# The order of the split buffers in the last column of a down stage

## The chip, the cores and the metric

The kernel runs on one core of a Trainium2 chip. The metric is the device time of one execution in microseconds; before the change it is 1727.62 us, the median of 3 runs (1727.11 to 1728.93). Times below are microseconds from the start of the profiled span unless marked otherwise.

## What is computed

One decoder layer on x of 256 rows (tokens) and 2048 columns, all float32: a feed-forward block (FFN 1), a mixer, a second feed-forward block (FFN 2), and a final norm. The two FFNs are alike, and they are what the change touches:

```python
def swiglu_ffn(x, w_gate, w_up, w_down):
    return (jax.nn.silu(x @ w_gate) * (x @ w_up)) @ w_down

x = x + 0.5 * swiglu_ffn(rms_norm(x, ffn1_norm[l]), ffn1_w_gate[l], ffn1_w_up[l], ffn1_w_down[l])
...
x = x + y @ w_out[l]
x = x + 0.5 * swiglu_ffn(rms_norm(x, ffn2_norm[l]), ffn2_w_gate[l], ffn2_w_up[l], ffn2_w_down[l])
return rms_norm(x, final_norm)
```

w_gate and w_up are 2048 x 5632, w_down is 5632 x 2048. Between the FFNs stands the mixer: one input projection (2048 x 5120), a gated recurrence in one half of the columns, a gated short convolution in the other, and an output projection.

## The kernel before

**Splitting.** Each weight tile is loaded as float32 (a raw tile), then split into a high part, rounded by ACT (`act.copy`, seen as CAST hi), and a low part, raw minus high, by VectorE (TENSOR_TENSOR lo). TensorE multiplies with both: of a unit of four blocks of 128 rows by 512 columns, each of the two row tiles t takes 8 matmuls with the high part and 4 with the low part, 24 in all. `parts_of` (line 259) does a split in one piece, `low_part` (252) the low part alone.

**Pairs.** The high and low tile of one split are a pair. There are three pairs while the layout is "three", two in the layouts "two" and "fine" (line 187 on). Each pair is a pool of its own, allocated one after the other on the left side of SBUF: in "three" a pair has four blocks (8 KB high and 8 KB low per partition), in "fine" five blocks (10 KB and 10 KB). A stage opens its pools when the one before has closed its own, at the same base address, so the fine stage's pair0 lies over all of the pair0 of "three" and over the first 4 KB of its pair1's high tile; the fine pair1 lies over the rest of pair1 and over the high tile of pair2. A new tile waits for the last reader of the tiles whose place it takes.

**Which pair.** `split_tiles` (244) asks `least_recent` (213) for a pair. It takes the pair that was given out longest ago, or, while the list `plan` has entries, the one that stands first in it. The order of use is kept in `recent["pair"]`. Entering "two" keeps the order of labels 0 and 1; entering "fine" from a down stage sets it to 0, 1 and returning to "three" sets it to 0, 1, 2 (lines 1184 to 1189). Raw tiles rotate in the same way over raw0, raw1 and raw2, without a plan.

**An FFN** (`ffn`, 577) goes: the first blocks of gate and up (three units of hidden columns); then for s = 1 and 3 a down stage, which takes the hidden units so far into the residual, and a fine stage (`fine_blocks`, 1164), which makes the next four; then a last down stage. So there are three down stages in each FFN, of three, four and four hidden units, and two fine stages in each FFN, that is four fine stages in the kernel.

**A down stage** (`down`, 884) works on the four columns of 512 of w_down. Column 0 comes first, by `product` (400), unit after unit. Then columns 1 and 2 together, by `seven` (471), a scheme of seven products for two units, with the remaining units multiplied in the usual way. Its splits come in the order p0, p4, x01, p5, x11, p6, p2, x00, p3, x10, p1 (with three units in all, x11 and x10 are missing). Last comes column 3, again by `product`, and here the plan is used: lines 910 to 912. With four units, column 0 takes pairs 0, 1, 2, 0 and the eleven splits of `seven` follow, so that p3 is in pair0, x10 in pair1 and p1 in pair2 when column 3 begins.

With four units, the plan before gives the other two pairs in the order of use, the first of them again, then pair2: 0, 1, 0, 2. With three units it gives the two and pair2. In FFN 1 that is 0, 1, 2. In FFN 2 it is 1, 0, 2: the last plan of FFN 1 leaves pair1 used longer ago than pair0, and the mixer (layout "two", 40 splits in turn), the output projection and the first part of FFN 2 carry this order on.

**A fine stage** begins with a gate block. `block` (1037) writes out an order by hand (the list `steps`, line 1109 on), which holds on every engine: high of p0, low of p0, high of x01, the sum of w12 into w11 ("add"), high of p4, low of x01, low of p4, and so on; on PE p0 into bank a (15 matmuls: 10 with the high part, 5 with the low), p4 into bank c (15), x01 into banks e and c, p5 into a, x11 into e and c. Names in the profile: p0, p4, p5 are hi_g_p and lo_g_p, x01 and x11 are hi_g_x and lo_g_x (these lie elsewhere, in the pool "bigs"), w11, w12, w21, w22 are raw_g_w; the banks are ps_g_a, ps_g_c and ps_g_e. In a down stage the units of columns 0 and 3 are hi_d, lo_d and ps_d; the splits of `seven` are hi_d_p, lo_d_p, hi_d_x, lo_d_x with the banks ps_d_a, _c, _d, _e. Products p3 and x10 write banks a and d, p1 writes d.

**Order on the engines.** Outside the written-out order, instructions of an engine are put in order when the program is built, by when they are expected to be ready; each engine then runs its own in that order. Loads are issued by SP, whose instructions wait in its queue in order too. The fourth unit of column 3 takes the raw buffer of the first (raw0), and w11 of the fine stage, loaded into kept0, follows it on SP; w12 and x01 of the fine stage lie over raw0, w22 over raw1 and raw2. All lines of the profile read L43, since every operation is issued through a helper there; groups are told apart by tile names.

## Time and profile before

| | |
|---|---|
| median of the runs | 1727.62 us |
| the profiled execution, whole | 1730.88 us |
| its span, first to last instruction | 1729.1 us |
| granted TensorE clock, mean | 0.997 |
| PE busy | 1713.1 us (99%) |
| VectorE busy | 1506.5 us (87%) |
| ACT busy | 1093.9 us (63%) |
| DMA queue q1, share of 16 engines | 56.0% |

In a row of a timeline stand the start, the duration, the engine, the line, the operation, out<-in by tile names, the shape and the count of merged instructions; in brackets the idle time before it and what ended it. In a row by windows stand the stretch, its length, then the busy time of the engines PE, PEld, DVE, ACT, POOL with counts, the granted TensorE clock, the DMA share and GB/s. A row of PE's waits has the total, the number of times and the longest. A row of a DMA issue ends with the KB and the median time to landing.

### The profile page before, as it was taken

What the parts mean: (1) busy time and instruction counts of PE and PEld (TensorE: products, weight loads), DVE (VectorE), ACT (ScalarE), POOL (GpSimd) and SP (SyncE); (2) the same over time, 40 slices, a digit from 0 to 9 for tenths busy, and PEclk for the clock granted to TensorE, in tenths of its full rate; (3) what the DMA queues carried; (4) which work ended last, traced back from release to release, by engine and by line L of the source; (5) the groups of instructions that cost most, each with busy time, mean ns of one, the idle gap of its engine ahead of it and who ended that gap; (6) DMA issues with size and microseconds to landing.
All of it is one profiled execution on the core that took longest, in us unless ns stands there. A gap on an engine that the chain in (4) does not pass through costs nothing.

```text
span 1729.1 us, 20387 instructions
## 1 busy us (share of the span) xinstructions
PE 1713.1 (99%) x7937; PEld 1426.2 (82%) x7937; DVE 1506.5 (87%) x1290; ACT 1093.9 (63%) x1344; POOL 45.6 (3%) x78
## 2 busy tenths in 40 slices
PE   9999999999999999999999999999999999999998
PEld 8888888888788888888888888888788888788876
DVE  7989899988799978787997888888999986999886
ACT  7666566656576656667876666655666654666654
POOL 0010000000000000000000000000000000000000
PEclk9999999999999999999999999999999999999999
DMA  7765877765687675655556675765877656877653
GB/s 283 236 221 188 278 228 234 231 234 202 212 266 224 203 242 200 214 184 181 172 195 214 200 258 155 220 222 184 303 239 225 213 173 245 249 234 237 229 167 122
DMA packets 181584, 376.78 MB, mean 218 GB/s; under 512 B 7413, under 2 KB 10353, under 8 KB 177777
## 3 DMA queue, kind: packets, MB, share of 16 engines
q1 hardware_dynamic: 174656, 340.81, 56.0%
q0 software_dynamic: 6656, 33.63, 10.5%
q8 instruction: 62, 1.02, 0.2%
q10 hardware_dynamic: 176, 1.06, 0.2%
q14 instruction: 34, 0.27, 0.0%
HBM read 339.82 MB, written 2.10 MB: 198 GB/s over the span
## 4 chain that ended last, share of the span: by engine, by line
PE 94%; DVE 3%; issue 1%; ACT 1%; DMA 1%; DVEq 0%; ACTq 0%
PE ps_d L43 13%; PE ps_in L43 10%; PE ps_u_a L43 10%; PE ps_g_a L43 9%; PE ps_u_c L43 6%; PE ps_g_c L43 6%; PE ps_d_a L43 5%; PE ps_u_d L43 4%; PE ps_g_d L43 4%; PE ps_d_c L43 3%; PE ps_o L43 3%; PE ps_d_d L43 3%; PE ps_u_e L43 3%; PE ps_g L43 2%; PE ps_g_e L43 2%; PE ps_u L43 2%
## 5 line engine op out<-in xcount | busy, mean ns | idle before, releaser
L43 ACT CAST hi_g_p<-raw_g_w 128x1024 fp32r<-128x1024 f32 x112 | 138.4, 1263 | 101.5 <-PE ps_d L43 29.5
L43 DVE TENSOR_TENSOR lo_g_p<-raw_g_w,hi_g_p 128x2560 fp32r<-128x2560 f32 (+2 forms) x72 | 158.3, 2224 | 33.8 <-ACT hi_g_p L43 31.0
L43 ACT CAST hi_u_p<-raw_u_w 128x1024 fp32r<-128x1024 f32 x112 | 137.9, 1261 | 63.0 <-PE ps_u_a L43 20.9
L43 DVE TENSOR_TENSOR lo_u_p<-raw_u_w,hi_u_p 128x2560 fp32r<-128x2560 f32 (+2 forms) x72 | 158.9, 2226 | 12.1 <-ACT hi_u_p L43 11.2
L43 PE MATMUL ps_d<-hi_d,h 128*128 128x512 f32 x696 | 166.1, 390 | 0.0
L43 PEld LDWEIGHTS ps_d<-hi_d,h 128*128 128x128 f32 x696 | 130.0, 188 | 26.7
L43 ACT CAST hi_d<-raw_d 128x1024 fp32r<-128x1024 f32 x88 | 87.5, 1047 | 68.9 <-DMA raw_d<-in_ffn_w_down_dram 34.8
L43 PE MATMUL ps_in<-xT_nm,hi_in 128*128 128x512 f32 x512 | 122.5, 391 | 0.0
L43 DVE TENSOR_TENSOR lo_d<-raw_d,hi_d 128x2048 fp32r<-128x2048 f32 x44 | 99.7, 2287 | 22.6 <-ACT hi_d L43 22.5
L43 PEld LDWEIGHTS ps_in<-xT_nm,hi_in 128*128 128x128 f32 x512 | 94.0, 188 | 18.9 <-ACT tha L43 0.5
L43 ACT CAST hi_d_p<-raw_d 128x1024 fp32r<-128x1024 f32 x84 | 84.8, 1047 | 35.6 <-DVE raw_d L43 24.7
L43 DVE TENSOR_TENSOR lo_d_p<-raw_d,hi_d_p 128x2048 fp32r<-128x2048 f32 x42 | 95.1, 2284 | 7.5 <-ACT hi_d_p L43 7.4
L43 DVE TENSOR_TENSOR lo_in<-raw_in,hi_in 128x2048 fp32r<-128x2048 f32 x32 | 73.2, 2288 | 21.2 <-ACT hi_in L43 20.8
L43 PE MATMUL ps_d<-lo_d,h 128*128 128x512 f32 x348 | 86.2, 389 | 0.0
L43 ACT CAST hi_in<-raw_in 128x1024 fp32r<-128x1024 f32 x64 | 64.2, 1046 | 33.9 <-PE ps_in L43 19.9
L43 PEld LDWEIGHTS ps_d<-lo_d,h 128*128 128x128 f32 x348 | 65.3, 188 | 13.6
L43 DVE TENSOR_TENSOR raw_g_w<-raw_g_w,raw_g_w 128x1024 f32<-128x1024 f32 (+2 forms) x40 | 68.8, 1754 | 1.8 <-DMA raw_g_w<-in_ffn_w_gate_dram 1.3
L43 DVE TENSOR_TENSOR raw_u_w<-raw_u_w,raw_u_w 128x1024 f32<-128x1024 f32 (+2 forms) x40 | 68.8, 1753 | 0.6
L43 PEld LDWEIGHTS ps_in<-xT_nm,lo_in 128*128 128x128 f32 x512 | 65.6, 191 | 2.5
L43 PE MATMUL ps_in<-xT_nm,lo_in 128*128 128x256 f32 x512 | 66.4, 283 | 0.0
L43 PE MATMUL ps_u_a<-hi_u_p,x 128*128 128x512 f32 x224 | 57.5, 393 | 0.0
L43 PE MATMUL ps_g_a<-hi_g_p,x 128*128 128x512 f32 x224 | 56.6, 389 | 0.0
(503 smaller groups left out, 3953.3 us busy)
## 6 DMA issues: line engine op xcount, KB each, us to landing
raw_d<-in_ffn_w_down_dram SPq DMA_DIRECT2D x88, 1024.0 KB, 5.2
raw_g_w<-in_ffn_w_gate_dram SPq DMA_DIRECT2D x32, 1024.0 KB, 5.6
raw_u_w<-in_ffn_w_up_dram SPq DMA_DIRECT2D x32, 1024.0 KB, 5.7
raw_in<-in_w_in_dram SPq DMA_DIRECT2D x32, 1024.0 KB, 5.0
raw_g_x<-in_ffn_w_gate_dram SPq DMA_DIRECT2D x32, 768.0 KB, 6.9
raw_u_x<-in_ffn_w_up_dram SPq DMA_DIRECT2D x32, 768.0 KB, 7.5
raw_u<-in_ffn_w_up_dram SPq DMA_DIRECT2D x23, 1024.0 KB, 5.3
raw_g<-in_ffn_w_gate_dram SPq DMA_DIRECT2D x22, 1024.0 KB, 5.1
```

The source lines that it names most:

```text
L43: ins = getattr(self.engine, name)(*args, **kwargs)
```

## The change

The plan of column 3 is written as a constant. For four units it is 1, 0, 1, 2; for three units its last three, 0, 1, 2.

```diff
                 for c in (0, 3):
                     if c == 3:
-                        others = [i for i in recent["pair"] if i != 2]
-                        plan.extend(others + others[: len(us) - 3] + [2])
+                        plan.extend([1, 0, 1, 2][4 - len(us) :])
                     end = last and tag == 2 and c == NC_D - 1
                     ps = product(
                         wd, c, us[:-2] + [n, m], hidden.get, f"d{tag}_{m}_{c}", end,
```

So in the four-unit columns (two in each FFN) the order 0, 1, 0, 2 becomes 1, 0, 1, 2: the first unit takes the pair of x10, the second the pair of p3, the third the pair of the first unit, the fourth the pair of p1 as before. In the three-unit column of FFN 1 nothing changes. After the last column of FFN 1 the order of use is 0, 1, 2 in place of 1, 0, 2, and what follows carries the labels 0 and 1 exchanged as far as the three-unit column of FFN 2.

## The prediction

> **What bounds the kernel now.** First the page: its span and the chain of work that ended last.

> ```profile
> span 1729.1 us, 20387 instructions
> PE 94%; DVE 3%; issue 1%; ACT 1%; DMA 1%; DVEq 0%; ACTq 0%
> ```

> The end is set by TensorE, so only what makes PE wait counts. Second, the view of PE's waits, for those that repeat:

> ```profile
> PE ps_g_c L43 <- DVE lo_g_p L43: 2.5, 3, 0.9
> PE ps_g_c L43 <- ACT s_g L43: 1.3, 3, 0.4
> ```

> Two waits come three times each, in ps_g_c, the second bank of a fine stage's first gate block. There are four fine stages. Third, the view by windows: its first answer covers each fine stage from its first matmul to the start of product x11, its second (PE alone, first two rows) the whole stage.

> ```profile
> 202.19:216.47 14.28, 14.28 (x65) 11.82 (x63) 12.31 (x10) 8.51 (x9) 1.02 (x2) 1.00 0.92 240
> 451.31:467.83 16.52, 15.17 (x64) 11.59 (x63) 16.45 (x13) 10.75 (x10) 1.77 (x2) 1.00 0.80 207
> 1214.57:1231.09 16.52, 15.18 (x64) 11.59 (x63) 16.45 (x13) 9.44 (x9) 1.75 (x2) 1.00 0.92 271
> 1465.56:1482.09 16.53, 15.21 (x64) 11.59 (x63) 16.46 (x13) 10.78 (x10) 1.76 (x2) 1.00 0.81 207
> ...
> 202.19:365.39 163.20, 163.20 (x734) 1.00 0.76 238
> 451.31:616.76 165.45, 164.10 (x734) 1.00 0.75 235
> ```

> The four run the same code. The first takes 14.28 us without an idle moment; the others take 16.52, 16.52 and 16.53, at a granted clock of 1.00 in all. The whole stages differ by the same 2.25 (165.45 - 163.20): what is lost at the start is not made up, and nothing else is lost.

> Fourth, the timelines of ACT, PE and DVE, for why the first escapes.

> ```profile
> 191.51 2.43 ACT L43 CAST hi_g_p<-raw_g_w 128x1024 fp32r<-128x1024 f32 x2 [1.37 <-PE ps_d L43]
> ...
> 446.07 2.43 ACT L43 CAST hi_g_p<-raw_g_w 128x1024 fp32r<-128x1024 f32 x2 [10.70 <-PE ps_d L43]
> ...
> 1209.33 2.43 ACT L43 CAST hi_g_p<-raw_g_w 128x1024 fp32r<-128x1024 f32 x2 [6.73 <-PE ps_d L43]
> ```
> ```profile
> 191.31 3.79 PE L43 MATMUL ps_d<-hi_d,h 128*128 128x512 f32 x16
> 194.94 1.98 PE L43 MATMUL ps_d<-lo_d,h 128*128 128x512 f32 x8
> ...
> 440.44 3.79 PE L43 MATMUL ps_d<-hi_d,h 128*128 128x512 f32 x16
> 444.06 1.98 PE L43 MATMUL ps_d<-lo_d,h 128*128 128x512 f32 x8
> ```
> ```profile
> 195.19 2.83 DVE L43 TENSOR_TENSOR lo_g_p<-raw_g_w,hi_g_p 128x2560 fp32r<-128x2560 f32 x1 [2.73 <-PE ps_d L43]
> 198.05 2.89 DVE L43 TENSOR_TENSOR raw_g_w<-raw_g_w,raw_g_w 128x1024 f32<-128x1024 f32 x2
> ...
> 202.53 2.88 DVE L43 TENSOR_TENSOR lo_g_p<-raw_g_w,hi_g_p 128x1024 fp32r<-128x1024 f32 x2
> ...
> 451.39 2.89 DVE L43 TENSOR_TENSOR raw_g_w<-raw_g_w,raw_g_w 128x1024 f32<-128x1024 f32 x2
> ```

> A unit is 24 matmuls, one each 0.227 ((444.06 - 440.44) / 16), so 5.44. The cast of product p0 into the fine stage's pair0 starts 0.2 after a unit of column 3 ends. In the first stage (order 0,1,2) that is the first unit, ended at 191.31, 10.7 before the fine stage's first matmul. In the second (0,1,0,2) it is the third, ended at 444.06 + 8 x 0.227 = 445.88, which used pair0 again: 5.2 before. In the third (order 1,0,2: the mixer and output stages leave the labels 0 and 1 swapped) it is the second of three. From this cast the chain is p0's low part, the sum into w11 (DVE), p4's cast, p4's low part. The sum starts 4.14 ahead of PE in the first stage (198.05 to 202.19) and 0.08 behind it in the second (451.39 to 451.31): 4.22 later. In the first stage p4's low part ends at 205.41. PE has 25 matmuls ahead of p4's low products (p0's 15 and p4's 10 high ones), so their second half is due at 202.19 + 27 x 0.227 = 208.32, 2.9 later. 4.22 less 2.9 is 1.3: the wait that PE shows at each of the other three, (2.5 + 1.3) / 3.

> **The change, part by part.** No instruction, byte or tile is added; only which of three buffers a cast writes, and so what it waits for.

> *Four-unit columns (two in each FFN): 0,1,0,2 becomes 1,0,1,2.* The last three uses are then 0,1,2, as ahead of the first fine stage. p0's cast may start after the second unit, at 440.44 + 0.19, 5.44 earlier, its low part after the third unit's high products, at 444.31; the sum at 447.17, 4.14 ahead of PE, exactly as in the first stage. Two fine stages follow such columns: 2 x 2.24 (16.52 - 14.28), from both sides 1.3 (the waits that PE names, (2.5 + 1.3)/3) and 2.25 (the whole stage). I take 2.24, since identical code shows it.

> *Three-unit columns.* FFN 1: still 0,1,2, nothing moves before the second down stage. FFN 2: the last four-unit plan of FFN 1 now leaves the labels as 0,1, not 1,0. The mixer takes the two in turn, 40 times; everything there is the same with the names exchanged, and FFN 2's first column comes out as 0,1,2: another 2.24, between 0 and 2.25 because this part rests on the count alone.

> *What it costs: the first unit's cast waits for a later product*, x10 in place of p3, four times. At the second down stage:

> ```profile
> 420.61 2.00 ACT L43 CAST hi_d<-raw_d 128x1024 fp32r<-128x1024 f32 x2 [1.58 <-PE ps_d_a L43]
> 427.96 2.00 ACT L43 CAST hi_d<-raw_d 128x1024 fp32r<-128x1024 f32 x2 [5.35 <-DMA raw_d<-in_ffn_w_down_dram]
> 430.89 2.00 ACT L43 CAST hi_d<-raw_d 128x1024 fp32r<-128x1024 f32 x2 [0.93 <-DMA raw_d<-in_ffn_w_down_dram]
> 433.38 2.00 ACT L43 CAST hi_d<-raw_d 128x1024 fp32r<-128x1024 f32 x2 [0.49 <-PE ps_d L43]
> ```
> ```profile
> 425.02 1.07 PE L43 MATMUL ps_d_a<-lo_d_x,h 128*128 128x512 f32 x4
> ...
> 429.56 3.79 PE L43 MATMUL ps_d<-hi_d,h 128*128 128x512 f32 x16
> ```

> x10's high products end where its low ones start, 425.02; the cast runs 425.21 to 427.21, due at 429.56: 2.35 to spare, in ACT's idle 5.35. Behind it on ACT stands only the second unit's cast, which waits for its load until 427.96 anyway.

> ```profile
> 422.65 2.29 DVE L43 TENSOR_TENSOR lo_d<-raw_d,hi_d 128x2048 fp32r<-128x2048 f32 x1
> ...
> 433.53 4.49 DVE L43 TENSOR_TENSOR lo_d<-raw_d,hi_d 128x2048 fp32r<-128x2048 f32 x2
> ```
> ```profile
> 417.71 7.62 SPq L43 DMA_DIRECT2D raw_d<-in_ffn_w_down_dram  x3
> 425.39 11.37 SPq L43 DMA_DIRECT2D raw_g_w<-in_ffn_w_gate_dram  x4
> ```
> ```profile
> raw_d<-in_ffn_w_down_dram SPq DMA_DIRECT2D x1, 1024.0 KB, 5.8
> raw_g_w<-in_ffn_w_gate_dram SPq DMA_DIRECT2D x1, 1024.0 KB, 8.1
> ...
> raw_g_w<-in_ffn_w_gate_dram SPq DMA_DIRECT2D x2, 1024.0 KB, 6.6
> ```

> Its low part moves from 422.65 to 427.3 and ends at 429.6, due at 429.56 + 3.62. That frees the raw buffer 4.65 later, and the fourth unit's load waits for it on SP, with the fine stage's w11 right behind (the last raw_d row ends at 425.33, raw_g_w follows at 425.39). Unit four: issued 429.6, landed 435.4 (5.8), cast behind unit three's, low part done at 440.0; due at 445.88. w11: issued 430.0, landed 438.2 (8.1), wanted at 440.6. w12 takes unit four's buffer, free at 435.8 before (the first of the two low parts from 433.53; unit four was cast at 430.89, ahead of unit three) and at 440.0 now, so it lands at 446.6 (6.6); the sum wants it at 447.17, and PE feels it 2.9 later. All of it is hidden: the cast by p1's products, the loads by units one to four. The thinnest cover is the 2.35 on ACT; the same code runs in all four columns, and without that cover each us late costs one in each.

> **Sum:** 3 x 2.24 = 6.7. The profiled execution took 1730.88 (span 1729.1 and 1.8 around it) and becomes 1724.2; the median of the runs is 3.26 below it: 1727.62 - 6.7 = **1720.9 us**.

> **Rivals.**

> *The first unit's cast falls behind the second's on ACT* (the order on the engine is set when the program is built, and this one is now ready later). It would run from 429.96, its first half done at 431.0: PE waits 1.45 at each of four columns. What that costs depends on the clock; the kernel has one wait of about that size:

> ```profile
> 1664.91 1.98 PE L43 MATMUL ps_d_a<-hi_d_p,hs 128*128 128x512 f32 x8
> 1666.72 0.39 PE L43 MATMUL ps_d_e<-hi_d_x,h 128*128 128x512 f32 x1
> 1668.90 1.91 PE L43 MATMUL ps_d_a<-lo_d_p,hs 128*128 128x512 f32 x4 [1.79 <-DVE lo_d_p L43]
> 1670.61 2.67 PE L43 MATMUL ps_d_e<-hi_d_x,h 128*128 128x512 f32 x7
> 1673.12 1.99 PE L43 MATMUL ps_d_c<-hi_d_x,h 128*128 128x512 f32 x8
> ```
> ```profile
> 1666.00:1672.00 6.00, 4.21 (x13) 0.76 0.50 175
> ```

> Twenty matmuls took 8.21 where 20 x 0.227 = 4.54 are due: a wait of 1.79 cost 3.67, since the granted clock fell to 0.76 in those 6 us, while the fine stages' waits of 0.83 left it at 1.00. So: if the clock holds, 4 x 1.45 = 5.8 back, 1726.7; if it falls in that proportion (x 2.05), 4 x 2.97 = 11.9 back, **1732.8, slower**. It decides once that cast ends over 2.35 later than I put it. For it: ACT's four casts above already stand in order of readiness. Against: x10's release (425.2) is 2.7 ahead of the second unit's load.
> [...]

> *The bubble is a lack of room, not of order*: p4's pair1 or the next load takes the place of pair0 at once, and it stays at 1727.6. [...] The first fine stage, with the same buffers and no gap, speaks against.

> *The loads behind SP come late*: w12 at 8.1 in place of 6.6 is harmless; at 2.9 beyond the sum's start each further us costs one. A part of 2 x 2.24 is lost: 1721 to 1725.

> *FFN 2's first column keeps its order*: 1727.62 - 4.5 = 1723.1.

> *Another wait like that at 1668.90 comes or goes*, as the build orders the rest anew: 1724.6 or 1717.2.

> **How the numbers follow.** Forecast 65%; the cast behind its neighbour 10% (7 with the clock lost, 3 without); no room 4%; late loads 6%; two places only 7%; a wait more 4%, one less 4%. What this measurement can tell from no change is 0.2%, 3.5 us: below 1724.2 is faster. Faster: 65 + 7 + 4 and 4 of the late loads, 80%. Same: 3 + 4 + 4 and 2 of the late loads, 13%. Slower: 7%. The forecast alone would be 1720.0 to 1723.7 (three times 1.3 above; half the runs' spread of 1.8 below). With the partial cases, a wait more, and half of the way to a wait less, the range is 1718.5 to 1726.0.

> **What would show it.** In the changed profile: p0's cast of the second, third and fourth fine stage starts some 10.7 ahead of that stage's first matmul, all four windows last 14.28, and the two repeated waits are gone from PE's list. The first unit's cast in four-unit columns waits for x10 and ends before the column's first matmul. Up to the second down stage's last column nothing differs. I am wrong if PE waits at a column's start, or if a fine stage still takes 16.5 with p0's cast early.

## The result and the profile after

The changed kernel takes 1725.08 us (median of 22 runs, 1722.86 to 1728.15) against 1727.89 for the kernel before (22 runs, 1726.68 to 1731.07): a ratio of 0.9984 with a 95% interval of 0.9977 to 0.9990, or 2.8 us less. 6.7 us less were forecast. The profiled execution took 1727.47.

The page of the changed kernel, its span, the chain that ended last by engine, and that chain's lines:

```profile
span 1725.5 us, 20385 instructions
...
PE 77%; issue 5%; DMA 5%; DVE 2%; ACT 1%; SPq 0%; POOL 0%; DVEq 0%; POOLq 0%; ACTq 0%
PE ps_in L43 10%; PE ps_u_a L43 9%; PE ps_d L43 8%; PE ps_g_a L43 8%; PE ps_u_c L43 6%; PE ps_g_c L43 4%; PE ps_u_d L43 4%; PE ps_g_d L43 4%; PE ps_d_a L43 4%; PE ps_o L43 3%; DMA raw_g_w<-raw_g_w 2%; PE ps_d_c L43 2%; PE ps_u_e L43 2%; PE ps_d_d L43 2%; PE ps_g_e L43 2%
```

The chain went from 94% PE to 77%, and a transfer has joined it: raw_g_w<-raw_g_w, a DMA from SBUF to SBUF that adds one weight tile into another. The waits of PE in the changed kernel:

```profile
PE ps_g_e L43 <- DVE lo_g_x L43: 3.4, 2, 1.8
PE ps_d_a L43 <- DVE lo_d_p L43: 2.3, 2, 1.8
```

The two waits that came three times each in ps_g_c are gone. In their place stands one that comes twice: ps_g_e waiting for the low part of x11. By windows of the changed kernel, first the four starts, from a fine stage's first matmul to the start of x11, then the four whole stages (PE alone, with granted clock, DMA share and GB/s behind it):

```profile
200.76:215.04 14.28, 14.28 (x65) 11.82 (x63) 12.30 (x10) 8.51 (x9) 1.02 (x2) 1.00 0.92 240
449.85:464.13 14.28, 14.28 (x65) 11.82 (x64) 13.61 (x11) 5.75 (x7) 1.78 (x2) 1.00 0.97 256
1211.64:1225.92 14.28, 14.28 (x64) 11.82 (x63) 11.04 (x9) 8.00 (x8) 1.72 (x2) 1.00 1.05 302
1462.44:1476.72 14.28, 14.28 (x64) 11.82 (x63) 10.23 (x10) 5.76 (x7) 1.77 (x2) 1.00 0.97 251
```
```profile
200.76:363.96 163.20, 163.20 (x734) 1.00 0.76 239
449.85:613.45 163.60, 163.49 (x733) 1.00 0.77 240
1211.64:1376.97 165.33, 163.50 (x733) 1.00 0.76 242
1462.44:1627.52 165.08, 163.52 (x734) 1.00 0.76 238
```

And the last two stages of the kernel before, whose first two are in the prediction:

```profile
1214.57:1380.01 165.44, 164.10 (x733) 1.00 0.76 242
1465.56:1631.01 165.45, 164.12 (x733) 1.00 0.75 235
```

All four starts now last 14.28, at a granted clock of 1.00 and without an idle moment, as the prediction said. But the whole stages gained 0, 1.85, 0.11 and 0.37, in sum 2.3 and not 6.7: what the start won in FFN 2 (third and fourth stage) was lost behind it, within the same stage. The second stage lost 0.40 of its 2.24, at the first matmul of p6, the product that reads w12 with w22 added (+18.6; times with a plus are counted from a fine stage's first matmul).

Where it went is seen in the third stage. VectorE, PE and POOL of the changed kernel, and its DMA issues there (KB each, median us from issue to landing):

```profile
1219.80 2.88 DVE L43 TENSOR_TENSOR lo_g_p<-raw_g_w,hi_g_p 128x1024 fp32r<-128x1024 f32 x2
1226.08 2.83 DVE L43 TENSOR_TENSOR raw_g_w<-raw_g_w,raw_g_w 128x2560 f32<-128x2560 f32 x1 [3.41 <-DMA raw_g_w<-in_ffn_w_gate_dram]
1228.83 1.75 DVE L43 TENSOR_TENSOR lo_g_x<-raw_g_x,hi_g_x 128x1536 fp32r<-128x1536 f32 x1
```
```profile
1227.28 1.52 PE L43 MATMUL ps_g_c<-hi_g_x,x 128*128 128x512 f32 x6
1230.63 0.96 PE L43 MATMUL ps_g_e<-lo_g_x,x 128*128 128x512 f32 x3 [1.83 <-DVE lo_g_x L43]
```
```profile
1213.38 0.86 POOL L1070 DMA_DIRECT2D raw_g_w<-raw_g_w  x1 [50.16 <-DVE lo_g_x L43]
1214.92 0.86 POOL L1070 DMA_DIRECT2D raw_g_w<-raw_g_w  x1 [0.69 <-DMA raw_g_w<-in_ffn_w_gate_dram]
```
```profile
raw_g_w<-in_ffn_w_gate_dram SPq DMA_DIRECT2D x1, 1024.0 KB, 12.2
raw_g_w<-raw_g_w POOLq DMA_DIRECT2D x1, 1024.0 KB, 10.9
raw_g_x<-in_ffn_w_gate_dram SPq DMA_DIRECT2D x1, 768.0 KB, 14.3
raw_g_w<-in_ffn_w_gate_dram SPq DMA_DIRECT2D x1, 256.0 KB, 13.7
```

The same spot in the kernel before, where the stage starts at 1214.57:

```profile
1225.94 2.88 DVE L43 TENSOR_TENSOR lo_g_p<-raw_g_w,hi_g_p 128x1024 fp32r<-128x1024 f32 x2
1228.85 2.83 DVE L43 TENSOR_TENSOR raw_g_w<-raw_g_w,raw_g_w 128x2560 f32<-128x2560 f32 x1
```
```profile
1218.14 1.75 POOL L1071 DMA_DIRECT2D raw_g_w<-raw_g_w  x2 [52.02 <-DMA raw_g_x<-in_ffn_w_gate_dram]
```
```profile
raw_g_w<-in_ffn_w_gate_dram SPq DMA_DIRECT2D x1, 1024.0 KB, 7.2
raw_g_w<-in_ffn_w_gate_dram SPq DMA_DIRECT2D x1, 256.0 KB, 7.4
```

Read it from the end. PE is through with x11's high part at 1228.80 (1227.28 + 1.52) and gets its low part at 1230.58 (1228.83 + 1.75). That low part stands on VectorE behind the sum of w21 into w11 (2560 wide), and the sum waited 3.41 for w21's load, the two rows from SP. In the kernel before this load took 7.2 and 7.4, and the sum followed the low part of p5 at once. Now it took 12.2 and 13.7. It could not be issued earlier: SP waits there for PE's ps_d, that is for the last unit of the down stage, so in both kernels it goes out some 0.2 us after the stage's first matmul. What did move is POOL's accumulate, w12 += w22, whose two DMAs wait for the sum of w12 into w11 and for w22. The sum became 4.2 earlier, as wanted, and so the accumulate was issued 1.7 and 3.3 after the stage's first matmul (1213.38 and 1214.92 less 1211.64) in place of 3.6 and 4.1: beside w21's load and no longer behind most of it.

That is a reading of one trace. The experiments test it against another: that the loads are late because the whole queue of loads now runs closer to PE (a **backlog**), whoever shares the DMA engines. A third candidate is x00's load (768 KB), which follows w21 on SP: it moved as well, in the second to fourth stage from +4.7 to between +1.2 and +1.9.

### The profile page after: what moved, and what is told of

It reads as the page before. It is cut to its first block, busy times and chain, and to the rows that moved or that the text cites. A ratio compares the mean times of both kernels' runs of the same rounds, so it can differ in the third digit from the quotient of the medians.

```text
span 1725.5 us, 20385 instructions
## 1 busy us (share of the span) xinstructions
PE 1708.7 (99%) x7937; PEld 1424.3 (83%) x7937; DVE 1506.8 (87%) x1290; ACT 1093.3 (63%) x1344; POOL 45.7 (3%) x78
## 3 DMA queue, kind: packets, MB, share of 16 engines
q8 instruction: 62, 1.02, 0.2%
## 4 chain that ended last, share of the span: by engine, by line
PE 77%; issue 5%; DMA 5%; DVE 2%; ACT 1%; SPq 0%; POOL 0%; DVEq 0%; POOLq 0%; ACTq 0%
PE ps_in L43 10%; PE ps_u_a L43 9%; PE ps_d L43 8%; PE ps_g_a L43 8%; PE ps_u_c L43 6%; PE ps_g_c L43 4%; PE ps_u_d L43 4%; PE ps_g_d L43 4%; PE ps_d_a L43 4%; PE ps_o L43 3%; DMA raw_g_w<-raw_g_w 2%; PE ps_d_c L43 2%; PE ps_u_e L43 2%; PE ps_d_d L43 2%; PE ps_g_e L43 2%
## 5 line engine op out<-in xcount | busy, mean ns | idle before, releaser
L43 ACT CAST hi_g_p<-raw_g_w 128x1024 fp32r<-128x1024 f32 x112 | 137.9, 1262 | 69.5 <-PE ps_g_a L43 16.4
L43 ACT CAST hi_u_p<-raw_u_w 128x1024 fp32r<-128x1024 f32 x112 | 137.8, 1261 | 62.0 <-PE ps_u_a L43 20.9
L43 DVE TENSOR_TENSOR lo_g_p<-raw_g_w,hi_g_p 128x2560 fp32r<-128x2560 f32 (+2 forms) x72 | 158.5, 2225 | 20.5 <-PE ps_d L43 14.3
L43 DVE TENSOR_TENSOR lo_u_p<-raw_u_w,hi_u_p 128x2560 fp32r<-128x2560 f32 (+2 forms) x72 | 158.9, 2226 | 11.1 <-ACT hi_u_p L43 10.1
L43 PE MATMUL ps_d<-hi_d,h 128*128 128x512 f32 x696 | 166.1, 390 | 0.0
L43 PEld LDWEIGHTS ps_d<-hi_d,h 128*128 128x128 f32 x696 | 130.0, 188 | 26.7
L43 ACT CAST hi_d<-raw_d 128x1024 fp32r<-128x1024 f32 x88 | 87.4, 1047 | 72.5 <-PE ps_d_d L43 23.6
L43 PE MATMUL ps_in<-xT_nm,hi_in 128*128 128x512 f32 x512 | 122.5, 391 | 0.0
L43 DVE TENSOR_TENSOR lo_d<-raw_d,hi_d 128x2048 fp32r<-128x2048 f32 x44 | 99.7, 2288 | 23.8 <-ACT hi_d L43 23.7
L43 PEld LDWEIGHTS ps_in<-xT_nm,hi_in 128*128 128x128 f32 x512 | 94.0, 188 | 18.8 <-ACT tha L43 0.5
L43 ACT CAST hi_d_p<-raw_d 128x1024 fp32r<-128x1024 f32 x84 | 84.8, 1047 | 35.5 <-DVE raw_d L43 24.8
L43 DVE TENSOR_TENSOR lo_d_p<-raw_d,hi_d_p 128x2048 fp32r<-128x2048 f32 x42 | 95.0, 2284 | 7.4 <-ACT hi_d_p L43 7.4
L43 DVE TENSOR_TENSOR lo_in<-raw_in,hi_in 128x2048 fp32r<-128x2048 f32 x32 | 73.2, 2287 | 21.1 <-ACT hi_in L43 20.7
L43 PE MATMUL ps_d<-lo_d,h 128*128 128x512 f32 x348 | 86.2, 389 | 0.0
L43 ACT CAST hi_in<-raw_in 128x1024 fp32r<-128x1024 f32 x64 | 64.2, 1048 | 33.4 <-PE ps_in L43 18.0
L43 PEld LDWEIGHTS ps_d<-lo_d,h 128*128 128x128 f32 x348 | 65.3, 188 | 13.6
L43 DVE TENSOR_TENSOR raw_g_w<-raw_g_w,raw_g_w 128x1024 f32<-128x1024 f32 (+2 forms) x40 | 68.8, 1753 | 8.6 <-DMA raw_g_w<-in_ffn_w_gate_dram 8.2
L43 DVE TENSOR_TENSOR raw_u_w<-raw_u_w,raw_u_w 128x1024 f32<-128x1024 f32 (+2 forms) x40 | 68.8, 1753 | 0.6
L43 PEld LDWEIGHTS ps_in<-xT_nm,lo_in 128*128 128x128 f32 x512 | 65.6, 191 | 2.5
L43 PE MATMUL ps_in<-xT_nm,lo_in 128*128 128x256 f32 x512 | 66.4, 283 | 0.0
L43 ACT CAST hi_g_x<-raw_g_x 128x1536 fp32r<-128x1536 f32 x32 | 47.2, 1474 | 21.6 <-DMA raw_g_x<-in_ffn_w_gate_dram 20.3
L43 PE MATMUL ps_u_a<-hi_u_p,x 128*128 128x512 f32 x224 | 57.5, 393 | 0.0
## 6 DMA issues: line engine op xcount, KB each, us to landing
raw_d<-in_ffn_w_down_dram SPq DMA_DIRECT2D x88, 1024.0 KB, 5.2
raw_g_w<-in_ffn_w_gate_dram SPq DMA_DIRECT2D x32, 1024.0 KB, 5.8
raw_u_w<-in_ffn_w_up_dram SPq DMA_DIRECT2D x32, 1024.0 KB, 5.8
raw_in<-in_w_in_dram SPq DMA_DIRECT2D x32, 1024.0 KB, 5.0
raw_u<-in_ffn_w_up_dram SPq DMA_DIRECT2D x23, 1024.0 KB, 5.4
raw_g<-in_ffn_w_gate_dram SPq DMA_DIRECT2D x22, 1024.0 KB, 5.2
```

What stands on the lines that cost most here:

```text
L43: ins = getattr(self.engine, name)(*args, **kwargs)
```

## The experiments

**The changed kernel again.**

> The changed kernel once more, on the chip of the runs that follow. Both theories: about 2.8 us below the kernel before (ratio 0.998), the four windows from a fine stage's first matmul to product x11 at 14.28 us, and PE waits on lo_g_x of x11 between 0 and 1.9 us in the second to fourth fine stage, differing from execution to execution, since they hang on when w21 lands (7.9 to 14.3 us after the fine stage's first matmul in the profile of the change).

Measured: 1724.41 us (11 runs, 1722.63 to 1727.34), before on that chip 1728.69 (20 runs): 0.9979, interval 0.9970 to 0.9987. That is 4.3 us less where some 2.8 was expected, with overlapping intervals. The starts last 14.28 in all four stages, the waits on x11's low part are 1.45 and 1.70, at the same two places. The waits repeat.

**Without the accumulate.** The first gate block of a fine stage issues no accumulate.

```diff
-(-2.1, gather_sum),
+(-2.1, gather_sum if b else lambda: None),
```

> The changed kernel without the POOL accumulate w12 += w22 in the first gate block of each fine stage (that sum, and so product p6's half with w22, is left out there). Contention theory (the accumulate, 1.25 MB moved inside SBUF, now starts together with w21's load and they share the 16 DMA engines): w21 lands 5 to 8 us after the stage's first matmul in all four stages, no PE wait on lo_g_x is left, and the time is what the prediction asked for, 1727.9 - 6.7 = 1721 us (ratio 0.996). Backlog theory (w21 is late because the fourth unit's load and the fine stage's loads behind it on SP were issued up to 4.6 us later): w21 still lands at 10 to 14, the waits of 1.5 us or more stay, ratio 0.998.

Measured: 1721.89 us (5 runs, 1721.05 to 1722.84), 0.9964 (0.9952 to 0.9977), that is 6.8 us less than before. The whole stages, by windows of PE:

```profile
202.40:365.60 163.20, 163.20 (x734) 1.00 0.71 230
451.42:614.62 163.20, 163.20 (x733) 1.00 0.73 233
1212.78:1375.98 163.20, 163.20 (x733) 1.00 0.73 237
1461.56:1624.76 163.20, 163.20 (x734) 1.00 0.72 232
```

w21 lands between +5.9 and +8.3 in all four (in the first at +5.9, where it landed at +12.0 both before and after the change), and PE does not wait in any of them. It is issued no earlier, the loads ahead of it are the same, and x00's load still goes out at +1.2 to +1.8. So neither the backlog nor x00's load makes w21 late by itself: it takes the accumulate. And the forecast's own sum, 3 x 2.24, comes out in full once that is gone.

**The sum behind x11.** Nothing is left out here; the sum of w21 goes behind x11's low part on VectorE, in the first gate block alone.

```diff
-(11.2, lambda: add("w21", all5)),
+(11.2 if b else 14.05, lambda: add("w21", all5)),
```

> The changed kernel with one step moved: in the first gate block of each fine stage the sum of w21 into w11 stands on DVE behind x11's low part, not ahead of it. Queue theory (PE waits only because x11's low part stands behind the waiting sum on DVE): w21 still lands as late as 14, the sum still waits for it, but lo_g_x ends some 13 us after the stage's first matmul, PE does not wait, 1721 us (ratio 0.996). If the late w21 itself, or the accumulate that p6 needs, is what binds PE: another wait of 1 to 2 us takes its place at lo_g_p of p6 or later, ratio 0.998.

Measured: 1721.50 us (5 runs, 1721.22 to 1723.84), 0.9965 (0.9951 to 0.9978). VectorE and PE in the fourth stage, which starts at 1459.91:

```profile
1470.58 1.75 DVE L43 TENSOR_TENSOR lo_g_x<-raw_g_x,hi_g_x 128x1536 fp32r<-128x1536 f32 x1
1474.31 2.83 DVE L43 TENSOR_TENSOR raw_g_w<-raw_g_w,raw_g_w 128x2560 f32<-128x2560 f32 x1 [1.97 <-DMA raw_g_w<-in_ffn_w_gate_dram]
```
```profile
1475.55 1.52 PE L43 MATMUL ps_g_c<-hi_g_x,x 128*128 128x512 f32 x6
1476.91 0.84 PE L43 MATMUL ps_g_e<-lo_g_x,x 128*128 128x512 f32 x3
```

w21 is as late here as in the changed kernel (the sum waits for it until 1474.31, +14.4), but x11's low part is done at 1472.33, and PE goes from one row to the next without a wait. In the third stage w21 landed at +10.7, earlier than before the move. The four stages take 163.20, 163.47, 163.61 and 163.20. So the late w21 cost PE its 1.5 to 1.8 through the low part queued behind the sum. The 0.27 and 0.41 that are left lie at p6's first matmul.

**The accumulate later.** It is held on POOL until the snapshot s1 of bank a, by a copy of one column; x11 keeps its place.

```diff
+pool = Engine(tc, nc.gpsimd)
+pool.held = b == 0
+if b == 0:
+    pool.tensor_copy(held_at[:, :1], snaps["s1"][:, :1])
...
-(-2.1, gather_sum),
+(-2.1 if b else 3.46, gather_sum),
```

> The changed kernel with the accumulate of the first gate block held on POOL until bank a's snapshot s1, some 4.2 us after the stage's first matmul (before the change it started at 3.6, after it at 0.2 to 3.3). Contention theory: w21 lands at 5 to 8 again, as before the change, no wait on lo_g_x, 1721 us (ratio 0.996), with the accumulate landing at 14 to 16. Backlog theory: as the changed kernel, 0.998.

Measured: 1724.08 us (10 runs, 1722.17 to 1726.60), 0.9974 (0.9965 to 0.9984). The accumulate goes out around +6, w21 lands at +6.0 to +8.3 and the waits on x11 are gone, which is the contention undone. The median did not follow. The waits of PE, and ACT in the third stage (start 1212.14):

```profile
PE ps_g_a L43 <- ACT u_g L43: 1.4, 2, 0.8
```
```profile
1227.24 1.05 ACT L43 CAST hi_g_p<-raw_g_w 128x1024 fp32r<-128x1024 f32 x1 [4.76 <-DMA raw_g_w<-raw_g_w]
1228.46 2.42 ACT L43 CAST hi_g_p<-raw_g_w 128x1536 fp32r<-128x1536 f32 x2 [0.17 <-DMA raw_g_w<-raw_g_w]
1230.79 0.59 ACT L43 ACTIVATE u_g<-ps_g_a 128x512 f32<-128x512 f32 x1
```

Now the accumulate is late for its own reader: p6's cast waits 4.76 for it, the snapshot u_g stands behind that cast on ACT, and PE waits until the snapshot has read bank a. Held this long, the accumulate is the transfer that comes late: the stages take 163.23, 163.21, 164.29 and 164.19, so 2.1 us are lost in place of the changed kernel's 4.4.

**Held for a shorter time.** The same hold, released by x01's low part instead of s1.

```diff
-    pool.tensor_copy(held_at[:, :1], snaps["s1"][:, :1])
+    pool.tensor_copy(held_at[:, :1], f32(parts["x01"][1])[:, 0, :1])
...
-(-2.1 if b else 3.46, gather_sum),
+(-2.1 if b else -0.3, gather_sum),
```

> The changed kernel with the accumulate held on POOL for less long: until x01's low part, so that it starts some 2 us after the stage's first matmul (6.0 in the run that held it to the snapshot, where p6 then waited up to 0.8 for it). Contention theory: w21's last piece lands at 8 to 11, the sum and lo_g_x come in time, the accumulate lands by 14.5 and p6 does not wait: 1721.5 to 1722.5 us (ratio 0.9965). If the accumulate's own length under contention binds PE either way: 1723.5 to 1724.5, with waits at p6.

Measured: 1723.06 us (5 runs, 1721.89 to 1723.55), 0.9963 (0.9950 to 0.9975). The accumulate goes out at +1.5 to +2.6; w21 lands at +6.8, +8.1, +13.3 and +6.7. The wait in the fourth stage is gone, in the third 0.85 is left. The stages take 163.23, 163.23, 164.37 and 163.45, so by the windows of this one profile the hold saves most of the 4.4 (1.5 is left). The time lies between the two forecasts and decides for neither; the wait that is left is at x11, not at p6.

**Control: the moved sum alone**, with the plan of the kernel before.

> Control: the kernel before, with the same step moved (the sum of w21 behind x11's low part in the first gate block of each fine stage). In the kernel before the sum does not wait for a load, and the waits at lo_g_p of p4 and at the snapshot come earlier than both: all theories expect ratio 1.000 (1728 us) and windows of 14.3, 16.5, 16.5 and 16.5. If instead the move alone brings a gain, it, and not the order of the pairs, made the gain of the run with the sum behind x11.

Measured: 1728.74 us (11 runs, 1727.17 to 1729.48) against 1729.12 (19 runs), 0.9997 (0.9988 to 1.0006). Its waits of PE:

```profile
PE ps_g_c L43 <- DVE lo_g_p L43: 2.5, 3, 0.9
...
PE ps_g_c L43 <- ACT s_g L43: 1.3, 3, 0.4
```

They are those of the kernel before, to the digit. The move is worth nothing without the change.

**FFN 2's three-unit column in the old order**, on top of the moved sum.

```diff
-plan.extend([1, 0, 1, 2][4 - len(us) :])
+plan.extend([1, 0, 2] if tag == 2 and len(us) == 3 else [1, 0, 1, 2][4 - len(us) :])
```

> The changed kernel with the sum behind x11, but with FFN 2's three-unit column in the order it had before (1, 0, 2). The prediction's step on the three-unit column: its fine stage, the third, takes 16.5 again to product x11 with p0's cast after the second unit, the other three 14.28, and the time is 2.2 above the run with the sum behind x11 (1723.7 against 1721.5, ratio 0.9975). If the labels do not matter: 14.28 in all and 1721.5.

Measured: 1725.10 us (9 runs, 1723.16 to 1727.10), 0.9977 (0.9967 to 0.9986). By windows of PE:

```profile
200.28:363.48 163.20, 163.20 (x733) 1.00 0.77 239
449.39:612.59 163.20, 163.20 (x733) 1.00 0.77 240
1210.99:1376.43 165.44, 164.10 (x734) 1.00 0.77 242
1461.92:1625.15 163.23, 163.23 (x734) 1.00 0.77 241
```

Only the third stage is back at 165.44, with the two old waits (0.85 and 0.42) in it and nowhere else. The exchange of labels through the mixer does give the third place, and it is worth 165.44 - 163.20 = 2.24 where nothing eats it.

**The moved sum again**, beside these two.

> The changed kernel with the sum behind x11 once more: ratio 0.9962 to 0.9968, some 1721.5 us, PE waits on lo_g_x in no fine stage, whatever w21's landing is. If the first run was luck with the landings: up to 1725.

Measured: 1721.85 us (5 runs, 1721.04 to 1723.86), 0.9960 (0.9947 to 0.9972). The stages take 163.20, 163.39, 163.97 and 163.60; the longest wait left in them is 0.46, in the third, at p6's product. What these runs lose there goes with the accumulate's landing: 0.03 with its last piece landing at +15.2 (short hold, second stage), 0.27 at +15.5 and 0.77 at +16.0. Against the control on the same chip the change of plan is worth 1728.74 - 1721.85 = 6.9 us. The median lies 3.25 below that of the old order in FFN 2, more than 2.24, but the two intervals (to 0.9972 and from 0.9967) overlap, so the time alone doesn't size that place; the windows do.

## Why the prediction was right in part

**The bubble and its cause: right.** p0's cast now starts as the second of the four units ends, two units ahead of the fine stage. ACT of the changed kernel, from the second down stage's last column on:

```profile
423.75 2.00 ACT L43 CAST hi_d<-raw_d 128x1024 fp32r<-128x1024 f32 x2 [6.15 <-PE ps_d_d L43]
...
439.16 2.43 ACT L43 CAST hi_g_p<-raw_g_w 128x1024 fp32r<-128x1024 f32 x2 [3.36 <-PE ps_d L43]
```

439.16 is 10.69 ahead of the stage's first matmul at 449.85 (10.7 was forecast), the two waits are gone and every start lasts 14.28. Lack of room, the rival, is out. (The step of 0.227 per matmul is 5.44 / 24; the quotient printed beside it in the prediction is 0.226. Nothing hangs on the difference.)

**The cost of the moved cast: right.** The first row is the first unit's cast, waiting for bank d of x10. Here is PE:

```profile
423.55 1.07 PE L43 MATMUL ps_d_a<-lo_d_x,h 128*128 128x512 f32 x4
...
428.08 3.11 PE L43 MATMUL ps_d<-hi_d,h 128*128 128x512 f32 x13
```

It starts 0.2 after x10's high products and ends at 425.75, 2.33 before the column's first matmul (2.35 forecast). No column starts with a wait, so the rival that put this cast behind its neighbour is out too. The labels of FFN 2: right, by the run that put the old order back.

**The size: wrong, and here is the step.** "2 x 2.24 (16.52 - 14.28) ... I take 2.24, since identical code shows it", and the third 2.24 for FFN 2. The sum 3 x 2.24 = 6.7 holds for the start of the stages and was carried over to their ends without following what the earlier start releases. Measured over the whole stages the three terms are 1.85, 0.11 and 0.37. "All of it is hidden: ... the loads by units one to four" went through w11, w12 and the fourth unit's load; w21 and POOL's accumulate are not in it, though the accumulate waits for the very sum whose 4.22 the forecast moved. Among the rivals, late loads came nearest (1721 to 1725), but it named w12 and SP. w12 came in time (landed at -5.6 in the second stage, with the sum at -4.1); what was late was w21, which was issued as early as before. All the signs that the prediction named for the columns and the fine stages came true, and none of them looked beyond the start of x11. 1725.08 lies inside its range of 1718.5 to 1726.0, near the end that it gave to partial cases, and not below 1724.2, to which it gave 80%.

The profile of before had the warning. The first stage, taken as the model of a stage without a gap, had its accumulate issued ahead of its start, and its VectorE shows this:

```profile
214.27 2.83 DVE L43 TENSOR_TENSOR raw_g_w<-raw_g_w,raw_g_w 128x2560 f32<-128x2560 f32 x1 [1.33 <-DMA raw_g_w<-in_ffn_w_gate_dram]
217.01 1.75 DVE L43 TENSOR_TENSOR lo_g_x<-raw_g_x,hi_g_x 128x1536 fp32r<-128x1536 f32 x1
```

The same wait for the same load, 1.33, ended with x11's low part done at 218.76; PE wants it at 216.47 + 12 x 0.227 = 219.19: 0.4 to spare. The model stage was itself 0.4 us from the new wait, and in the stages of FFN 2 w21 then landed 2 us later still (+14 against +12).

**A wait of 1.79 costs 3.67: not in general.** That figure, which carried the slow rival, came from one execution. The same wait stands in the last down stage of every profile here, 1.75 to 1.83 long. By windows of 6 us around it, the changed kernel's two profiled executions (in the columns PE, PEld, DVE, ACT, POOL, then granted clock):

```profile
1662.30:1668.30 6.00, 4.18 (x14) 3.00 (x13) 6.00 (x5) 3.33 (x4) 0.00 (x0) 0.84 0.51 175
```
```profile
1663.95:1669.95 6.00, 4.17 (x18) 3.11 (x17) 6.00 (x5) 3.33 (x4) 0.00 (x0) 1.00 0.50 175
```

With the clock at 1.00 the eight matmuls of ps_d_c that follow start 4.89 after the matmul ahead of the wait; in the other execution 6.17, 1.3 later, and take 2.29 in place of 1.98 themselves. So the same code lost some 1.6 us in one execution and not in the other. Four of the ten profiles lost it. In the two of them that are the kernel before and the changed kernel the clock stood at 0.50 for 3.41 us: by that an estimate of 1.7 us (half of 3.41) for each such drop, a fixed amount and not the prediction's factor of 2.05 on the wait.

**Nothing differs up to the second down stage: right in order, not in time.** The first down stage began at 138.62 in the profile of before and at 136.33 in that of the changed kernel; in the second profile of the same changed kernel it was 138.73. So of the 3.6 between the two spans (1729.1 - 1725.5) 2.3 lie ahead of the change and are not its doing; the 2.8 of the medians rests on 22 runs each. The ten profiles fall into two groups, whichever plan they have: in five the record of the granted clock starts its 1.00 at 4.0 to 5.4 (4.05 in the profile of the changed kernel) and the first down stage begins at 136.3 to 136.6, in five at 9.4 to 10.5 (10.24 in that of before) and at 138.3 to 138.7.

**What stays open.** In the second stage the accumulate was issued at +1.1 and w21 still landed at +7.9, in the third it was issued at +1.7 and w21 landed at +14.3; in the repeat again +8.1 against +13.9. Why the second stage gets away was not separated by a run of its own, but the profiles show a pattern. Where the accumulate went out ahead of w21 or within 0.1 us of it (the first stage, and the fourth with the new plan), w21 landed at +10.6 to +14.3. Where it went out at +1.1 to +1.8 in the first, second or fourth stage, w21 landed at +6.7 to +8.1. In the third stage of the new plan w21 landed at +10.7 to +14.3 with the accumulate at +1.7 to +3.6; there x11's load, ahead of w21 on SP, landed at +4.6 to +5.4, against +3.3 at the latest in the others.

## What to carry to other kernels

A stage without a gap is only a model for the others if its margins are known: follow it past the place where the gap was, to the next point where its engines wait for a load, and write down what is to spare there. When a step is moved, list everything that it releases on every queue, the accumulating DMAs of POOL too, and ask what shares the DMA engines with each (here POOL's queue took 50.6% of the 16 beside the loads' 53.7%). And on an engine that works in order, as VectorE did here (x11's low part stood behind a sum that waited 3.41), put the instruction that may wait for a load behind the one that TensorE needs first: here that one line turned a gain of 2.8 to 4.3 us into one of some 7.

## What the runs showed of the hardware

An accumulating DMA of 1.25 MB from SBUF to SBUF, issued from 0.9 us ahead of a load of the same size from HBM to 3.4 us behind it, could put that load's landing from between +5.9 and +8.3 (no accumulate) to between +10.6 and +14.3, though not in every stage, and itself landed some 8 to 15 us after its issue. In the third stage of the changed kernel the two shared the 16 DMA engines: from 1213 to 1225 the queue of SP's loads (q1) took 53.7% of them and that of POOL's accumulates (q0) 50.6%; from 1211 to 1214, with no packet of POOL's queue yet, SP's took 102.0%. Without the accumulate the two pieces of w21 landed 7.4 and 7.7 after their issue in that stage, in the changed kernel 12.2 and 13.7.

Waits of TensorE of one length had two prices. In the last down stage the wait of 1.75 to 1.83 left the clock at 1.00 in six of ten profiles and lowered it in four (the kernel before, the changed kernel, and the accumulate held longer and for a shorter time): from the end of the wait to the low products into ps_d_e these took 6.04 to 6.09, the six others 4.44 to 4.48. The waits of 1.45 to 1.83 in the fine stages left it at 1.00. By windows of PE in the kernel before, behind the wait that ended at 1668.90 (busy time, granted clock, DMA share and GB/s):

```profile
1669.12:1672.53 3.41, 3.41 (x9) 0.50 0.44 170
1672.53:1675.94 3.41, 3.41 (x16) 1.00 0.36 114
```
